# First half's layer norm by token, its swishes in other buffers, one projection and the bias rows moved

## The chip, the cores and the metric

The kernel runs on one core of a Trainium2 chip. The metric is the device time of one execution in microseconds (us): of the kernel before, three runs took 2139.2 (median), 2138.27 and 2141.2. The core has a matrix engine (TensorE, PE in the profile, with PEld for its weight loads), VectorE (DVE), ScalarE (ACT), GpSimd (POOL), and SyncE (SP), whose queue issues the transfers between the core and the chip's memory. Each engine works through its own list of instructions in order and waits at an instruction until what it needs is there; an instruction that waits holds up all behind it on that engine.

## The reference, cut to what matters

The model has two layers over 1024 tokens of 1024 features. Layer 0 is a convolution module and a gated feed-forward net, layer 1 dilated attention and the same kind of net. The change is in the convolution module and in the preparation of a bias table for the attention:

```
def layernorm(x, g, b):
    x32 = x.astype(jnp.float32)
    mu = jnp.mean(x32, axis=-1, keepdims=True)
    xc = x32 - mu
    var = jnp.mean(xc * xc, axis=-1, keepdims=True)
    y = xc * lax.rsqrt(var + EPS) * g.astype(jnp.float32) + b.astype(jnp.float32)
    return y.astype(x.dtype)

def conformer_conv(h, w_pw1, b_pw1, w_dw, b_dw, ln_g, ln_b, w_pw2, b_pw2):
    u = h @ w_pw1 + b_pw1
    a, gate = jnp.split(u, 2, axis=-1)
    u = a * jax.nn.sigmoid(gate)
    u = lax.conv_general_dilated(
        u, w_dw[:, None, :], window_strides=(1,), padding=[(CONV_WIDTH - 1, 0)],
        dimension_numbers=("NWC", "WIO", "NWC"), feature_group_count=CONV_CHANNELS) + b_dw
    u = jax.nn.silu(layernorm(u, ln_g, ln_b))
    return u @ w_pw2 + b_pw2
...
    bias = jnp.transpose(bias_table[t5_bucket(dist * dilation)], (2, 0, 1)).astype(jnp.float32)
...
    for i in range(DEPTH):
        h = rmsnorm(x, norm_mix[i])
        ...
        h = rmsnorm(x, norm_ffn[i])
        x = x + swiglu(h, ffn_w_gate[i], ffn_w_up[i], ffn_w_down[i])
```

## The kernel before, in words

All activations stand with features on the 128 partitions and tokens along the free axis, so a sum over features is a sum over partitions and over eight tiles. The 1024 tokens are worked in two halves of 512 (h = 0 and 1). Each projection is a `gemm`: weights and inputs are each split into a high and a low part, and three matmuls (lines 158, 159, 160) are issued for each of the eight blocks of 128 features, so one output tile takes 24 matmuls of 512 columns. Weights come through the SP queue (line 140), ACT casts the high part (line 127) and DVE or POOL subtract the low one (line 128).

The part that matters runs in this order in the code. `glu(1, c)` is the first projection with its gate for block c of the second half: two output tiles, 48 matmuls, then a sigmoid on ACT (line 382) and a product on DVE (line 389). `conv(0)` filters the first half: 31 taps, most on DVE (line 427), some on ACT and POOL (lines 418, 419), its sums in buffers called `ap` (four of them). `layernorm(0)` norms over the eight tiles `u` of the first half. `glu(1, 4)` is the last of those projections. `bias_rows` makes the rows of the attention's bias for three head groups. `pw2(0)` is the second projection of the first half, eight output tiles, 192 matmuls, added into x at line 504. Then comes the norm before the feed-forward net (`rstd`, lines 189 to 211, and `normed`, line 214) and the net itself, whose matmuls on the first half run beside `conv(1)`, the filter of the second half.

In `layernorm(0)` PE sums the eight tiles with a matrix of ones, which leaves each token's mean on all partitions (line 449, fp32, two passes each); DVE takes it off (line 451); ACT squares (line 472) into two buffers `ctmp` that take turns; PE sums the squares in the same way (line 473); ACT takes the root of a full tile (line 475) and DVE its reciprocal (line 479); DVE multiplies (line 483), ACT makes the swish into the two `ctmp` buffers (line 485), and DVE and POOL split it into high and low (lines 493, 495). `rstd` does it by token: DVE adds the squares (line 203), PE sums them into one column per 128 tokens (line 181, `colsum`), ACT and DVE work on 128x4 numbers (lines 208, 210), and PE spreads the four columns out again with an identity matrix (line 189, `rows`).

`bias_rows` does three times: load a one-hot table into a buffer `tmp` (SP, line 627), copy the heads' values beside it (DVE, line 630), one matmul (PE, line 632), negate the result into a second `tmp` (DVE, line 634), and write it out in 16 small transfers (SP, line 638), from which the attention reads its table later, from 1084.9 us on. There are four buffers `tmp`, handed out in the order of the code; the squares and the normed tiles of the feed-forward net's norm use the same four.

A scheduler orders the instructions of each engine by a model of their times, within the dependencies; `tc.issue_after(i)` puts the instructions of its block that run on the engine of i behind i on that engine. Before, `bias_rows` has its matmuls behind the last matmul of `glu(1, 4)`.

Of the kernel before, what the change touches and what calls it, by code (L numbers as in the profile page):

```python
# [12 lines left out]
F32 = mybir.dt.float32  # L13
F32R = mybir.dt.float32r
AF = mybir.ActivationFunctionType
ALU = mybir.AluOpType

P = 128
T = 1024
TH = 512  # L20
D = 1024
DC = D // P
# [64 lines left out]
def trunk(ctx, tc, xT, vecs, wdw, w1, w2, wqkv, wo, wg, wu, wd, rel, onehot, sel, outT, scratch, kept1):  # L87
    nc = tc.nc
# [7 lines left out]
    spool = ctx.enter_context(tc.tile_pool(name="spool", bufs=2))  # L96
# [6 lines left out]
    ones = const.tile([P, P], F32, name="ones")  # L103
    nc.vector.memset(ones, 1.0)
    epst = vec[:, NV : NV + 1]
# [44 lines left out]
    marks = {}  # L150
# [42 lines left out]
    def rstd(get, n, sc, pool=()):  # L193

        acc = sc.acc()[:, :n]
        for c in range(DC):
            sq = acc if c == 0 else sc.tmp()[:, :n]
            if c in pool:
                nc.gpsimd.tensor_tensor(out=sq, in0=get(c), in1=get(c), op=ALU.mult)
            else:  # L200
                nc.scalar.activation(sq, get(c), AF.Square)
            if c:
                nc.vector.tensor_tensor(out=acc, in0=acc, in1=sq, op=ALU.add)
        st = sc.st()
        colsum(st, acc, n)
        nj = n // P
        sd = spool.tile([P, 4], F32, name="sd")
        nc.scalar.activation(sd[:, :nj], st[:, 0:nj], AF.Sqrt, bias=epst, scale=1.0 / D)
        rs = spool.tile([P, 4], F32, name="rs")
        nc.vector.reciprocal(rs[:, :nj], sd[:, :nj])  # L210
        return rows(rs[:, :nj], n, sc)
# [108 lines left out]
    def conv_and_half_ffn():  # L320

        with ExitStack() as cs:
            cpool = cs.enter_context(tc.tile_pool(name="cpool", bufs=2))
# [45 lines left out]
            def glu(h, c, hl, bc=None, w=None):  # L369

                wb, wa = w or pw1_weights(c, True)
                pb = mm_ps()
                gemm(pb, wb, pairs(hl))
                pa = mm_ps()
                gemm(pa, wa, pairs(hl))
                if bc is not None:
                    tb, ta = tmp(), tmp()
                    nc.vector.tensor_tensor(out=tb, in0=pb, in1=bc, op=ALU.mult)
                    nc.vector.tensor_tensor(out=ta, in0=pa, in1=bc, op=ALU.mult)
                    pb, pa = tb, ta  # L380
                sg = tmp()
                nc.scalar.activation(sg, pb, AF.Sigmoid, bias=vec[:, V_B1 + DC + c : V_B1 + DC + c + 1])
                t = cpool.tile([P, KW - 1 + TH], F32, name="u", bufs=14)
                u[h, c] = t
                if h == 0:
                    nc.gpsimd.memset(t[:, : KW - 1], 0.0)
                else:
                    nc.scalar.copy(t[:, : KW - 1], u[0, c][:, TH:])
                nc.vector.scalar_tensor_tensor(
                    out=t[:, KW - 1 :],  # L390
                    in0=pa,
                    scalar=vec[:, V_B1 + c : V_B1 + c + 1],
                    in1=sg,
                    op0=ALU.add,
                    op1=ALU.mult,
                )
# [42 lines left out]
            def layernorm(h, sl, y):  # L439

                n = sl.stop - sl.start
                sc = csc[h]
                yh, yl = y
                vs = [u[h, c][:, sl] for c in range(DC)]
                if h == 0:

                    bc = sc.ps()[:, :n]
                    for c in range(DC):
                        nc.tensor.matmul(bc, ones, vs[c], start=(c == 0), stop=(c == DC - 1))
                    for c in range(DC):  # L450
                        nc.vector.scalar_tensor_tensor(
                            out=vs[c], in0=bc, scalar=-1.0 / D, in1=vs[c], op0=ALU.mult, op1=ALU.add
                        )
                else:
                    sv = sc.acc()[:, :n]
                    nc.vector.tensor_tensor(out=sv, in0=vs[0], in1=vs[1], op=ALU.add)
                    for c in range(2, DC):
                        nc.vector.tensor_tensor(out=sv, in0=sv, in1=vs[c], op=ALU.add)
                    st = sc.ps()
                    colsum(st, sv, n)  # L460
                    mu = spool.tile([P, 4], F32, name="mu")[:, : n // P]
                    nc.vector.tensor_scalar(
                        out=mu, in0=st[:, : n // P], scalar1=1.0 / D, scalar2=None, op0=ALU.mult
                    )
                    bc = rows(mu, n, sc)
                    for c in range(DC):
                        nc.vector.tensor_tensor(out=vs[c], in0=vs[c], in1=bc, op=ALU.subtract)
                if h == 0:
                    ps = sc.ps()[:, :n]
                    for c in range(DC):  # L470
                        sq = sc.tmp()[:, :n]
                        nc.scalar.activation(sq, vs[c], AF.Square)
                        nc.tensor.matmul(ps, ones, sq, start=(c == 0), stop=(c == DC - 1))
                    br = sc.acc()[:, :n]
                    root = nc.scalar.activation(br, ps, AF.Sqrt, bias=epst, scale=1.0 / D)
                    with tc.issue_after(root.ins):

                        nc.scalar.activation(spool.tile([P, 4], F32, name="sd")[:, 0:1], epst, AF.Silu)
                    nc.vector.reciprocal(br, br)
                else:  # L480
                    br = rstd(lambda c: vs[c], n, sc)
                for c in range(DC):
                    nc.vector.tensor_tensor(out=vs[c], in0=vs[c], in1=br, op=ALU.mult)
                    t = sc.tmp()[:, :n]
                    nc.scalar.activation(
                        t,
                        vs[c],
                        AF.Silu,
                        bias=vec[:, V_LNB + c : V_LNB + c + 1],
                        scale=vec[:, V_LNG + c : V_LNG + c + 1],  # L490
                    )
                    if h == 0:
                        nc.vector.tensor_copy(yh[:, c, sl], t)  # L493
                        eng = nc.vector if c % 2 else nc.gpsimd
                        eng.tensor_tensor(out=yl[:, c, sl], in0=t, in1=yh[:, c, sl].bitcast(F32), op=ALU.subtract)
                    else:
                        split(t, yh[:, c, sl], yl[:, c, sl], nc.vector if c % 2 else nc.gpsimd)
# [61 lines left out]
            conv(0, range(4))  # L559
            layernorm(0, whole, y)  # L560
            for c in range(LATE[0], LATE[1]):
                glu(1, c, hb)
            with tc.issue_after(marks["gemm"]):
                bias_rows()
            pw2(0, whole, y)
            for c in range(LATE[1], JOINT):
                glu(1, c, hb)
            ha = pair_slots()
# [783 lines left out]
```

## Time and profile before

| What | Value |
|---|---|
| Runs: median (lowest, highest) | 2139.2 us (2138.27, 2141.2) |
| Profiled execution: its time | 2142.52 us |
| Profiled execution: span of the instructions | 2140.7 us |
| Mean granted clock of TensorE | 0.988 of full speed |
| Busy share of PE, DVE, ACT, POOL | 97%, 63%, 39%, 25% |
| Chain that ended last, share by engine | PE 79%, DVE 9%, POOL 7% |

The profiled execution took 1.82 us more than its span and 3.32 us more than the median of the runs shown. The busy shares are averages; PE is busy nearly all the time, so what matters is where it isn't, and where it runs at the lower of its two clocks.

### The profile page before, as it was taken

What the parts mean: (1) busy time and instruction counts of PE and PEld (TensorE: products, weight loads), DVE (VectorE), ACT (ScalarE), POOL (GpSimd) and SP (SyncE); (2) the same over time, 40 slices, a digit from 0 to 9 for tenths busy, and PEclk for the clock granted to TensorE, in tenths of its full rate; (3) what the DMA queues carried; (4) which work ended last, traced back from release to release, by engine and by line L of the source; (5) the groups of instructions that cost most, each with busy time, mean ns of one, the idle gap of its engine ahead of it and who ended that gap; (6) DMA issues with size and microseconds to landing.
All of it is one profiled execution on the core that took longest, in us unless ns stands there. A gap on an engine that the chain in (4) does not pass through costs nothing.

```text
span 2140.7 us, 24625 instructions
## 1 busy us (share of the span) xinstructions
PE 2079.0 (97%) x9550; PEld 1681.0 (79%) x9550; DVE 1358.1 (63%) x1997; ACT 831.7 (39%) x1336; POOL 526.9 (25%) x322
## 2 busy tenths in 40 slices
PE   8999889999999999999999999999999999999997
PEld 6786677778887888888887777877888888888887
DVE  8997687997455433332663337489766666666665
ACT  6675366524323222211443434455322232222234
POOL 3984169921323222211230112130000000000003
PEclk9999899999999999999999999999999999999999
DMA  8232222222222223321231211122111111111112
GB/s 323 74 110 93 86 68 86 89 91 96 99 98 84 95 98 99 98 79 50 79 109 60 70 60 62 45 74 77 59 60 59 50 50 60 50 49 42 58 59 79
DMA packets 54778, 172.62 MB, mean 81 GB/s; under 512 B 6782, under 2 KB 12165, under 8 KB 54661
## 3 DMA queue, kind: packets, MB, share of 16 engines
q1 hardware_dynamic: 54084, 170.52, 24.0%
q8 instruction: 75, 1.23, 0.2%
q10 hardware_dynamic: 576, 0.52, 0.1%
q14 instruction: 43, 0.34, 0.1%
HBM read 159.22 MB, written 11.80 MB: 80 GB/s over the span
## 4 chain that ended last, share of the span: by engine, by line
PE 79%; DVE 9%; POOL 7%; issue 3%; ACT 2%; DMA 1%; SPq 0%; DVEq 0%; POOLq 0%; ACTq 0%
PE mm L158 12%; PE mm L160 12%; PE mm L159 12%; PE aux L158 6%; PE aux L160 6%; PE aux L159 6%; POOL ap L419 5%; PE mm L1031 4%; PE mm L1029 4%; PE mm L1030 4%; DVE cacc L427 2%; PE nps L1029 2%; PE nps L1030 2%; PE nps L1031 2%; PE att L768 1%
## 5 line engine op out<-in xcount | busy, mean ns | idle before, releaser
L158 PE MATMUL mm<-slot,wh 128*128 128x512 f32 x1184 | 467.5, 395 | 11.8 <-DVE slot L493 10.2
L159 PE MATMUL mm<-slot,wl 128*128 128x512 f32 x1184 | 465.9, 394 | 3.7 <-DVE wl L128 3.7
L160 PE MATMUL mm<-slot,wh 128*128 128x512 f32 x1184 | 462.4, 392 | 1.3 <-DVE slot L128 1.2
L128 POOL TENSOR_TENSOR wl<-ws,wh 128x1024 fp32r<-128x1024 f32 (+1 forms) x91 | 215.5, 2368 | 799.0 <-ACT wh L127 767.6
L127 ACT CAST wh<-ws 128x1024 fp32r<-128x1024 f32 (+1 forms) x190 | 195.6, 1030 | 346.2 <-PE mm L160 159.4
L158 PEld LDWEIGHTS mm<-slot,wh 128*128 128x128 f32 x1184 | 224.1, 189 | 64.7 <-DVE slot L493 12.1
L159 PEld LDWEIGHTS mm<-slot,wl 128*128 128x128 f32 x1184 | 224.1, 189 | 52.3 <-DVE wl L128 4.5
L160 PEld LDWEIGHTS mm<-slot,wh 128*128 128x128 f32 x1184 | 223.6, 189 | 49.5 <-DVE slot L128 2.1
L419 POOL TENSOR_TENSOR ap<-ap,m 128x512 f32<-128x512 f32 x156 | 224.7, 1474 | 55.2 <-ACT m L418 55.1
L128 DVE TENSOR_TENSOR wl<-ws,wh 128x1024 fp32r<-128x1024 f32 (+1 forms) x99 | 130.6, 1319 | 153.6 <-ACT wh L127 153.3
L427 DVE SCALAR_TENSOR_TENSOR cacc<-u,wd_sb,cacc 128x512 f32<-128x512 f32 x302 | 207.8, 743 | 0.1
L128 POOL TENSOR_TENSOR slot<-ws,slot 128x1024 fp32r<-128x1024 f32 x2 | 4.8, 2414 | 639.2 <-ACT slot L127 639.2
L158 PE MATMUL aux<-slot,wh 128*128 128x512 f32 x352 | 139.7, 397 | 7.7 <-DVE x L317 7.7
L418 ACT ACTIVATE m<-u,wd_sb 128x512 f32<-128x512 f32 x156 | 111.0, 722 | 77.4 <-POOL ap L419 77.2
L1029 PE MATMUL mm<-slot,wp 128*128 128x512 f32 x352 | 137.9, 392 | 2.8 <-DVE tmp L1095 2.3
L159 PE MATMUL aux<-slot,wl 128*128 128x512 f32 x352 | 138.7, 394 | 0.8 <-DVE wl L128 0.5
L160 PE MATMUL aux<-slot,wh 128*128 128x512 f32 x352 | 138.8, 394 | 0.0
L1030 PE MATMUL mm<-slot,wp 128*128 128x512 f32 x352 | 138.0, 392 | 0.2 <-DVE wp L128 0.2
L1031 PE MATMUL mm<-slot,wp 128*128 128x512 f32 x352 | 137.4, 392 | 0.0
L127 ACT CAST wp<-ws 128x512 fp32r<-128x512 f32 x110 | 67.8, 621 | 147.8 <-PE mm L1031 55.2
L946 DVE TENSOR_TENSOR x<-aux,x 128x512 f32<-128x512 f32 x144 | 98.3, 687 | 38.2 <-PE aux L160 37.0
L128 DVE TENSOR_TENSOR slot<-tmp,slot 128x512 fp32r<-128x512 f32 x58 | 95.6, 1651 | 29.9 <-ACT slot L127 29.7
(275 smaller groups left out, 3789.8 us busy)
## 6 DMA issues: line engine op xcount, KB each, us to landing
ws<-wd SPq DMA_DIRECT2D x66, 512.0 KB, 3.5
ws<-wu SPq DMA_DIRECT2D x64, 512.0 KB, 3.5
ws<-wg SPq DMA_DIRECT2D x62, 512.0 KB, 3.5
ws<-w SPq DMA_DIRECT2D x40, 512.0 KB, 4.8
ws<-wqkv SPq DMA_DIRECT2D x34, 512.0 KB, 3.5
ws<-wo SPq DMA_DIRECT2D x16, 384.0 KB, 3.0
kept<-slot SPq DMA_DIRECT2D x10, 512.0 KB, 6.0
ws<-kept SPq DMA_DIRECT2D x10, 512.0 KB, 5.1
```

Of the source, the lines that this page charges most:

```text
L127: a = nc.scalar.copy(hi, src)
L128: b = eng.tensor_tensor(out=lo, in0=src, in1=hi.bitcast(F32), op=ALU.subtract)
L158: nc.tensor.matmul(ps, wh[:, sl], xh, start=(k == 0), stop=False)
L159: nc.tensor.matmul(ps, wl[:, sl], xh, start=False, stop=False)
L160: mm = nc.tensor.matmul(ps, wh[:, sl], xl, start=False, stop=(k == kt - 1))
L418: nc.scalar.activation(m, src(c, k), AF.Copy, scale=wk)
L419: nc.gpsimd.tensor_tensor(out=a, in0=a, in1=m, op=ALU.add)
L427: nc.vector.scalar_tensor_tensor(out=a if k or late else u[h, c][:, :TH], in0=src(c, k), scalar=wk, in1=b if k == nv - 1 else a, op0=ALU.mult,
L946: eng.tensor_tensor(out=out, in0=a, in1=b, op=op)
L1029: nc.tensor.matmul(ps, wh, xh, start=start and k == 0, stop=False, skip_group_check=not start)
L1030: nc.tensor.matmul(ps, wl, xh, start=False, stop=False, skip_group_check=not start)
L1031: nc.tensor.matmul(ps, wh, xl, start=False, stop=k == 3, skip_group_check=not start)
```

## The change

There are four parts. In `layernorm(0)` the deviation is taken through `rstd`, by token, as the second half has it; the eight squaring matmuls, the root and reciprocal of a full tile go. The swishes of the first half go into the four `ap` buffers that the filter has done with. The matmuls of `glu(1, 4)` are queued on PE behind the last matmul of the mean (`marks["mean"]`). `bias_rows` stands behind `pw2(0)` in the code, and its matmuls are queued behind the last matmul of `pw2(0)`.

```diff
@@ layernorm
                     bc = sc.ps()[:, :n]
                     for c in range(DC):
-                        nc.tensor.matmul(bc, ones, vs[c], start=(c == 0), stop=(c == DC - 1))
+                        mm = nc.tensor.matmul(bc, ones, vs[c], start=(c == 0), stop=(c == DC - 1))
+                    marks["mean"] = mm.ins
...
-                if h == 0:
-                    ps = sc.ps()[:, :n]
-                    for c in range(DC):
-                        sq = sc.tmp()[:, :n]
-                        nc.scalar.activation(sq, vs[c], AF.Square)
-                        nc.tensor.matmul(ps, ones, sq, start=(c == 0), stop=(c == DC - 1))
-                    br = sc.acc()[:, :n]
-                    root = nc.scalar.activation(br, ps, AF.Sqrt, bias=epst, scale=1.0 / D)
-                    with tc.issue_after(root.ins):
-
-                        nc.scalar.activation(spool.tile([P, 4], F32, name="sd")[:, 0:1], epst, AF.Silu)
-                    nc.vector.reciprocal(br, br)
-                else:
-                    br = rstd(lambda c: vs[c], n, sc)
+                br = rstd(lambda c: vs[c], n, sc)
                 for c in range(DC):
                     nc.vector.tensor_tensor(out=vs[c], in0=vs[c], in1=br, op=ALU.mult)
-                    t = sc.tmp()[:, :n]
+                    t = cpool.tile([P, TH], F32, name="ap", bufs=4)[:, :n] if h == 0 else sc.tmp()[:, :n]
@@ conv_and_half_ffn
             layernorm(0, whole, y)
             for c in range(LATE[0], LATE[1]):
-                glu(1, c, hb)
+                with tc.issue_after(marks["mean"]):
+                    glu(1, c, hb)
+            pw2(0, whole, y)
             with tc.issue_after(marks["gemm"]):
                 bias_rows()
-            pw2(0, whole, y)
```

In the changed file the lines behind stand 1 to 12 lower: the multiplication is line 471, the swish 473, the split 481 and 483, the addition into x 492, and the bias rows' load, copy, matmul, negation and writes are lines 616, 619, 621, 623 and 627.

On SP the list changes between the weights of `pw2(0)` (`ws<-w`) and those of the net (`wg`, `wu`); `tmp<-onehot` is the load of a bias table, `scratch<-tmp` the writes of its rows:

```order
 L140 DMA ws<-w 128x1024 x5
-L627 DMA tmp<-onehot 33x384 x2
-L638 DMA scratch<-tmp 32x384 x32
-L627 DMA tmp<-onehot 33x384
-L638 DMA scratch<-tmp 32x384 x16
+L616 DMA tmp<-onehot 33x384
 L140 DMA ws<-w 128x1024 x3
```

The 48 writes and two of the loads went from ahead of the last weights of `pw2(0)` to behind the net's first four weights, where the list now has:

```order
+L616 DMA tmp<-onehot 33x384
+L627 DMA scratch<-tmp 32x384 x32
+L616 DMA tmp<-onehot 33x384
+L140 DMA ws<-wg 128x1024
+L627 DMA scratch<-tmp 32x384 x16
 L140 DMA ws<-wu 128x1024
```

The third table's load stands behind 32 writes. On DVE, at the end of `pw2(0)`, the kernel before has the last additions into x and the sum of squares `ssq` of the net's norm in turns:

```order
192 L504 SCALAR_TENSOR_TENSOR x_0_96<-mm,vec,x_0_96 128x512
193 L203 TENSOR_TENSOR ssq<-ssq,tmp 128x512
194 L504 SCALAR_TENSOR_TENSOR x_0_98<-mm,vec,x_0_98 128x512
195 L128 TENSOR_TENSOR wl<-ws,wh 128x1024
196 L203 TENSOR_TENSOR ssq<-ssq,tmp 128x512
197 L504 SCALAR_TENSOR_TENSOR x_0_100<-mm,vec,x_0_100 128x512
198 L203 TENSOR_TENSOR ssq<-ssq,tmp 128x512
199 L210 RECIPROCAL rs<-sd 128x4
```

The changed kernel has at the same place, from the last two additions into x on (`tmp<-aux` is the negation of a bias row, `tmp<-vec` the copy of the heads):

```order
185 L492 SCALAR_TENSOR_TENSOR x_0_98<-mm,vec,x_0_98 128x512
186 L128 TENSOR_TENSOR wl<-ws,wh 128x1024
187 L492 SCALAR_TENSOR_TENSOR x_0_100<-mm,vec,x_0_100 128x512
188 L623 TENSOR_SCALAR tmp<-aux 128x384
189 L619 COPY tmp<-vec 33x128
190 L623 TENSOR_SCALAR tmp<-aux 128x384
191 L619 COPY tmp<-vec 33x128
192 L623 TENSOR_SCALAR tmp<-aux 128x384
193 L203 TENSOR_TENSOR ssq<-ssq,tmp 128x512 x7
```

All seven additions of the squares went behind the three negations. On PE the three bias matmuls went from among the squares' matmuls (two of them) and the first matmuls of `pw2(0)` (one) to the place between the last matmul of `pw2(0)` and the `colsum` of the net's norm:

```order
954 L160 MATMUL mm<-slot,wh 128x512
955 L621 MATMUL aux<-tmp 128x384 x3
956 L181 MATMUL aux<-ones,ssq 128x1 x4
957 L189 MATMUL aux<-ident,rs 128x128 x4
958 L158 MATMUL mm<-slot,wh 128x512
```

## Rows read from the trace of the kernel before

**Rows 1.** Timeline of PE: start, length, instruction, [idle before, what ended it].

```profile
196.41 1.02 PE L449 MATMUL aux<-u,ones 128*128 128x512 f32 x2
200.04 1.02 PE L449 MATMUL aux<-u,ones 128*128 128x512 f32 x2
209.11 4.81 PE L473 MATMUL aux<-ctmp,ones 128*128 128x512 f32 x10
224.12 0.79 PE L158 MATMUL mm<-slot,wh 128*128 128x512 f32 x1 [10.20 <-DVE slot L493]
226.12 1.65 PE L632 MATMUL aux<-tmp 33*128 33x384 f32 x2
```

**Rows 2.** The same, from the end of `pw2(0)` to the net's first matmul.

```profile
272.50 0.39 PE L160 MATMUL mm<-slot,wh 128*128 128x512 f32 x1
277.04 1.87 PE L181 MATMUL aux<-ones,ssq 128*128 128x1 f32 x8 [4.15 <-DVE ssq L203]
279.47 2.08 PE L189 MATMUL aux<-ident,rs 128*128 128x128 f32 x8 [0.57 <-DVE rs L210]
283.04 0.80 PE L158 MATMUL mm<-slot,wh 128*128 128x512 f32 x1 [1.49 <-ACT slot L127]
```

**Rows 3.** Windows: length, busy of PE, PEld, DVE, ACT, POOL; PE's granted clock; DMA.

```profile
224.00:233.00 9.00, 8.88 (x19) 5.85 (x20) 7.34 (x12) 4.61 (x6) 4.18 (x4) 0.52 0.16 40
233.00:273.00 40.00, 39.89 (x176) 32.67 (x175) 19.89 (x22) 11.28 (x16) 3.36 (x2) 1.00 0.32 103
283.00:287.30 4.30, 4.26 (x10) 3.40 (x11) 4.30 (x7) 3.09 (x5) 3.98 (x3) 0.51 0.00 0
360.00:470.00 110.00, 99.70 (x416) 80.20 (x415) 110.00 (x140) 46.48 (x63) 71.53 (x42) 0.95 0.27 88
```

**Rows 4.** Timeline of DVE in `layernorm(0)` and in the bias rows.

```profile
195.41 0.69 DVE L437 TENSOR_TENSOR u<-cacc,ap 128x512 f32<-128x512 f32 x1
201.09 4.87 DVE L451 SCALAR_TENSOR_TENSOR u<-aux,u 128x512 f32<-128x512 f32 x8 [4.87 <-PE aux L449]
218.17 4.90 DVE L483 TENSOR_TENSOR u<-u,csv 128x512 f32<-128x512 f32 x8
228.40 0.55 DVE L634 TENSOR_SCALAR tmp<-aux 128x384 f32<-128x384 f32 x1
```

**Rows 5.** Timeline of DVE: additions of squares in a row, and the end of `pw2(0)`.

```profile
19.55 1.41 DVE L203 TENSOR_TENSOR ssq<-ssq,tmp 128x512 f32<-128x512 f32 x2
272.93 0.75 DVE L504 SCALAR_TENSOR_TENSOR x<-mm,vec,x 128x512 f32<-128x512 f32 x1 [2.48 <-PE mm L160]
281.58 2.72 DVE L214 SCALAR_TENSOR_TENSOR tmp<-x,vec,aux 128x512 f32<-128x512 f32 x4 [2.17 <-PE aux L189]
```

**Rows 6.** Timeline of PE early in the kernel, `colsum` and `rows` at the full clock.

```profile
25.27 0.95 PE L181 MATMUL aux<-ones,ssq 128*128 128x1 f32 x8
28.49 1.05 PE L189 MATMUL aux<-ident,rs 128*128 128x128 f32 x8
```

**Rows 7.** PE by lines from 224.3 to 272.7: count, busy us, mean ns.

```profile
L158 PE MATMUL mm<-slot,wh 128*128 128x512 f32 x64 | 26.7, 417 | 10.2 <-DVE slot L493 10.2
```

**Rows 8.** Timeline of SP's queue: start, length, transfers issued.

```profile
207.05 14.69 SPq L638 DMA_DIRECT2D scratch<-tmp  x32
221.83 0.32 SPq L627 DMA_DIRECT2D tmp<-onehot  x1
```

**Rows 9.** Transfers by line: count, KB each, median us from issue to landing.

```profile
scratch<-tmp SPq DMA_DIRECT2D x48, 48.0 KB, 1.6
```

**Rows 10.** Timeline of ACT between the squares and the root.

```profile
212.76 1.28 ACT L475 ACT_TABLE_LOAD   x1
214.06 0.69 ACT L475 ACTIVATE csv<-aux,vec 128x512 f32<-128x512 f32 x1
```

**Rows 11.** PE's waits: us in total, times, the longest.

```profile
PE aux L158 <- DVE x L317: 7.7, 2, 4.1
```

**Rows 12.** Timeline of DVE: three filter taps of `conv(1)` in a row.

```profile
383.48 2.06 DVE L427 SCALAR_TENSOR_TENSOR cacc<-u,wd_sb,cacc 128x512 f32<-128x512 f32 x3
```

## The prediction

> **What bounds the kernel now.** I read the timeline of PE first, since PE is busy nearly all the time and everything it doesn't do is seen as a gap there. Around the change it has two. At 224.12 the first matmul of `pw2(0)` waited 10.20 us for the cast of the first swish [rows 1]; the norm's chain through ACT and DVE stands in that gap. At 277.04 the `colsum` of the net's norm waited 4.15 us for DVE's last addition, and the net's first matmul came only at 283.04, though PE's last work had ended at 272.50 + 0.39 = 272.89 [rows 2]. The windows come second: after each gap PE runs at the lower clock (0.52 of full in the 9 us from 224, 0.51 in the 4.3 us from 283), and between them at full clock, with 176 matmuls in 39.89 us, 0.227 us each [rows 3]. So this stretch is bound by PE's work plus two chains that it waits for, and the change alters both chains. The third view is SP's queue: 32 writes of the bias rows took it 14.69 us, 0.46 us each, though one lands 1.6 us after its issue [rows 8, 9]. In the kernel before nobody waits for them.
>
> **The mean and the last first projection.** The last filter sum is done at 195.41 + 0.69 = 196.10 [rows 4]. Before, the two passes of the mean's last matmul began only at 200.04, behind matmuls of `glu(1, 4)`, and ended at 201.06 [rows 1]. Now nothing of `glu(1, 4)` is ahead of them: about 196.16 + 1.02 = 197.2, 3.9 us earlier. It isn't free: the matmuls that ran in between come afterwards, and PE idles for about 3 us in two pieces while it waits for the last two sums. All 48 of `glu(1, 4)` then run from 197.2 to 197.2 + 48 x 0.227 = 208.1, beside the norm, so PE's work is only moved. If the two pieces bring the lower clock, the 4.3 us at half speed from 283 say what that costs, about 2.1 us [rows 3]; the pieces are shorter than the 4.15 us that came before those, so I take nothing and keep 2.1 as the upper end.
>
> **The deviation by token.** DVE's eight subtractions take 4.87 us [rows 4], to 202.1. Seven additions follow at 0.72 (two took 1.41 with 0.69 for the second [rows 5]): 5.0 us, to 207.1, with ACT's squares in their shadow. That is before PE is free at 208.1, so `colsum` starts at 208.1. From `colsum` to the first use of the broadcast it was 281.58 - 277.04 = 4.54 us in the net's norm [rows 2, 5], at the lower clock; at the full one its two matmul groups take 0.95 and 1.05 instead of 1.87 and 2.08 [rows 2, 6], which leaves 2.6. PE comes here from unbroken work, so I take 2.9: the multiplications start at 211.0 (bounds 210.7 and 212.6), where they started at 218.17 [rows 4]. From there to PE's first matmul it was 224.12 - 218.17 = 5.95; DVE's list between is the same (eight multiplications, one product, a cast), so PE restarts at 217.0, 7.1 us earlier. The four buffers for the swishes bring the later tiles sooner, but PE was already busy for 8.88 of the 9 us after its restart [rows 3], so they are worth nothing beyond that; with two of them the cover would be the same slow clock.
>
> On the root there is a page to weigh. The row shows 1.28 us for the load of a table and the root 0.02 us behind it [rows 10]. The Trainium skill (ScalarE: Activation LUTs, What ACT_TABLE_LOAD costs) puts a drain of about 1.38 us on top of the load at every switch. By that the root would be some 0.5 us later and the whole 0.5 us longer; the row shows no such drain, and the sum goes by the row.
>
> **The second projection.** It is 3 x 64 = 192 matmuls (one of the three equal lines is shown [rows 7]), 192 x 0.227 = 43.6 us. Before, it lasted from 224.12 to 272.89 = 48.8, of which 1.65 was a bias matmul [rows 1]; so 3.6 us went to the lower clock. The bias matmul goes; I keep the 3.6, since a gap of similar length precedes (bounds 2.1, as after 283, and 4.3). `pw2(0)` then ends at E = 217.0 + 43.6 + 3.6 = 264.2, 8.7 us earlier.
>
> **The bias rows behind it.** Here a wait is added, and it is the largest term. From E: DVE's last addition into x takes 0.04 + 0.75 [rows 5], the first negation 0.55 [rows 4], so the first write is issued at E + 1.4. The second table was loaded ahead and its negation comes before SP needs it. 32 writes take SP 14.69 us [rows 8], to E + 16.1; only then does SP issue the third table's load. With the writes' 1.6 us to landing [rows 9] as the nearest row it is there at E + 17.8. PE stands at the third bias matmul, in front of its own `colsum`; that matmul takes 1.65 at the lower clock [rows 1], to E + 19.4, and the negation 0.55, to E + 20.0. Behind it on DVE stand all seven additions of the squares, 5.0 us: `colsum` at E + 25.1. (On ACT the squares wait too: the first two `tmp` they take are those whose writes must land, the second's at about E + 17.3, the third the one that the third bias matmul reads. So even without DVE's order the norm would start no earlier than that.) Before, it was E + 4.15 [rows 2]. From `colsum` to the net's first matmul I keep 283.04 - 277.04 = 6.0: the third group's 16 writes land by about E + 29, before the normed tile that takes their buffer. So the net starts at E + 31.1 = 295.3, where it started at 283.04: 12.3 us later. The cover of the bias rows before was 40 us of `pw2(0)`; it is gone.
>
> The Trainium skill (DMA: Bandwidth & Descriptors, Issuing engines are not separate DMA queues) says that what the sequencer spends on starting a DMA is usually small beside the DMA itself. Here one start is 0.46 and one landing 1.6 us, but 32 starts in a row are 14.69 and hide the landings, so rows and page differ in what counts. By the page the time would come out as the first rival.
>
> **Behind it.** `conv(1)`, its taps and the net move together, since both start from this norm. In the new order of DVE most of the net's instructions stand two taps earlier against `conv(1)`, 2 x 0.69 = 1.4 us [rows 12]. DVE is full from 360 to 470 and PE waits for it there (7.7 us for additions into x alone [rows 11]; 10.3 us idle in all [rows 3]), so PE may get back 0 to 4.5; I take 1. Nothing else in the rest moves but names of buffers and a few matmuls where PE had no gap.
>
> **The sum.** -8.7 to the end of `pw2(0)`, then 31.1 to the net's start instead of 10.15 (+21.0), -1.0: +11.3. The profiled execution took 2142.52, so 2153.8 by its own time; it is 3.32 above the median of the runs shown (2139.2), so I say 2150.5.
>
> **Rivals.** First: starting a write costs next to nothing when the queue has nothing else, and only landings count. Then the first negation is at E + 1.4, the second at 3.1, its writes land at 4.7 with the third table; matmul 0.9, negation 0.55, additions 5.0, `colsum` at E + 11.2 and the net at E + 17.2 = 281.4. That is -1.6 and -1.0 behind it: 2136.6, no change. For it: a write's data is only 48 KB. Against it: 0.46 us held through 32 writes in a row. 5%.
>
> Second, on the faster side: the bias rows hide here too, as their 48 writes did before, and the net's norm starts 10.15 us after E as it did. Then only the gain of the layer norm stands: -8.7 - 1.0, which gives 2129.5. It needs the third negation to be done before the additions are due, that is SP's 32 writes out by E; they can't begin before the first bias matmul, which stands behind the last of `pw2(0)`. From 11.3 us less of stall on, the change would be a gain. 7%.
>
> Third: the layer norm gives nothing back. The idle pieces at the mean drop the clock, `glu(1, 4)` and the chain run slow, and PE restarts about 224 as before; the stall of 21.0 then stands alone, with 1.0 back: 2159. For it: the clock fell after both gaps of rows 1 and 2. Against it: DVE's and ACT's chain is shorter whatever the clock. 6%.
>
> **How the numbers follow.** The forecast has 82%. Its own range: 2150.5 less 1.5 (shorter time at the lower clock), 3.5 (more given back behind) and 1 (landings), and plus 1.6 and 2.1 (slow clock in the chain and at the mean), 0.7 and 2 (longer slow stretches): not all at once, so 2144 to 2157. That leaves out the three rivals and the ends, 2 in 10. A measurement of this kernel tells 0.2%, about 4.3 us, from no change: faster than 2134.9 is the second rival, 7%; within is the first and the lowest end of the forecast, 6%; slower 87%.
>
> **What would show it.** PE: the mean's last matmul ends near 197, `pw2(0)` starts near 217 and ends near 264; a gap of about 16 us before the third bias matmul and one before `colsum`, and the net's first matmul near 295. SP: 32 writes of 0.46 us begin 1.4 us after `pw2(0)` and the third load stands behind them. DVE: seven additions behind the third negation. It is wrong if the third load lands before E + 10, if `colsum` comes under 15 us after `pw2(0)`, or if PE restarts after 221.

## The result and the profile after

The changed kernel took 2154.06 us (median of four runs, 2153.13 to 2154.93), the kernel before beside it 2140.2 (2138.27 to 2142.54): a ratio of 1.0062, 95% interval 1.0049 to 1.0075. It is slower by 13.9 us. The forecast was 2150.5, with 2144 to 2157 as its range. The profiled execution of the changed kernel took 2153.13 us, span 2151.3, mean granted clock 0.983; by profiled executions it is +10.6 over 2142.52, where the prediction had +11.3 and 2153.8. Of the two profiled executions the one before was the slowest of its four and the one after the fastest of its four, so the medians lie further apart than these two do.

First PE's timeline (start, length, instruction, [idle before, what ended it]), to be read beside [rows 1, 2]:

```profile
191.76 1.12 PE L449 MATMUL aux<-u,ones 128*128 128x512 f32 x2 [1.56 <-DVE u L437]
194.80 1.31 PE L449 MATMUL aux<-u,ones 128*128 128x512 f32 x2 [1.92 <-DVE u L437]
...
196.33 0.63 PE L159 MATMUL mm<-slot 128*128 128x512 f32 x1
...
208.30 0.95 PE L181 MATMUL aux<-ones,csv 128*128 128x1 f32 x8
209.91 1.13 PE L189 MATMUL aux<-ident,rs 128*128 128x128 f32 x8 [0.66 <-DVE rs L210]
217.08 0.76 PE L158 MATMUL mm<-slot,wh 128*128 128x512 f32 x1 [6.05 <-DVE slot L481]
...
263.21 0.39 PE L160 MATMUL mm<-slot,wh 128*128 128x512 f32 x1
263.53 0.91 PE L621 MATMUL aux<-tmp 33*128 33x384 f32 x2
267.28 1.60 PE L621 MATMUL aux<-tmp 33*128 33x384 f32 x2 [2.84 <-DVE tmp L619]
281.65 1.62 PE L621 MATMUL aux<-tmp 33*128 33x384 f32 x2 [12.78 <-DMA tmp<-onehot]
289.29 1.87 PE L181 MATMUL aux<-ones,ssq 128*128 128x1 f32 x8 [6.02 <-DVE ssq L203]
...
295.29 0.80 PE L158 MATMUL mm<-slot,wh 128*128 128x512 f32 x1 [1.49 <-ACT slot L127]
```

Down to 263.21 everything is earlier than before: the gap of 10.20 us at 224.12 is one of 6.05 at 217.08, and `pw2(0)` ends at E = 263.21 + 0.39 = 263.60 instead of 272.89. Then come gaps of 2.84, 12.78 and 6.02 us, where there was one of 4.15 [rows 2], and the net starts at 295.29 instead of 283.04: 12.25 us later.

What stands behind the two longest of them shows on SP's queue, on ACT and on DVE, each a timeline of the same stretch. SP:

```profile
265.06 14.70 SPq L627 DMA_DIRECT2D scratch<-tmp  x32
279.86 0.32 SPq L616 DMA_DIRECT2D tmp<-onehot  x1
```

ACT, the first three squares that the net's norm adds up:

```profile
273.63 0.63 ACT L201 ACTIVATE tmp<-x 128x512 f32<-128x512 f32 x1 [8.96 <-DMA scratch<-tmp]
281.05 0.63 ACT L201 ACTIVATE tmp<-x 128x512 f32<-128x512 f32 x1 [6.79 <-DMA scratch<-tmp]
283.31 0.63 ACT L201 ACTIVATE tmp<-x 128x512 f32<-128x512 f32 x1 [1.62 <-PE aux L621]
```

DVE, the filter's last sum, then the norm's subtractions, additions and multiplications, then the end of the projection:

```profile
194.06 0.69 DVE L437 TENSOR_TENSOR u<-cacc,ap 128x512 f32<-128x512 f32 x1
196.15 4.87 DVE L452 SCALAR_TENSOR_TENSOR u<-aux,u 128x512 f32<-128x512 f32 x8 [1.40 <-PE aux L449]
...
211.07 4.87 DVE L471 TENSOR_TENSOR u<-u,aux 128x512 f32<-128x512 f32 x8 [1.31 <-PE aux L189]
...
264.95 2.23 DVE L619 COPY tmp<-vec 33x128 f32<-33x128 f32 x1
268.92 0.56 DVE L623 TENSOR_SCALAR tmp<-aux 128x384 f32<-128x384 f32 x1 [1.74 <-PE aux L621]
269.39 0.21 DVE L619 COPY tmp<-vec 33x128 f32<-33x128 f32 x1
283.31 0.56 DVE L623 TENSOR_SCALAR tmp<-aux 128x384 f32<-128x384 f32 x1 [13.71 <-PE aux L621]
283.78 5.46 DVE L203 TENSOR_TENSOR ssq<-ssq,tmp 128x512 f32<-128x512 f32 x7
```

The 32 writes keep SP for 14.70 us, as they did before [rows 8], and the third load stands behind them; PE's wait of 12.78 ends with it. The seven additions stand in one row behind the third negation. In the kernel before, six of them were done one by one inside the projection, and only the seventh behind it; that is the one for which PE waited 4.15 us [rows 2].

Last the windows (length, then busy us of PE, PEld, DVE, ACT and POOL with counts, the granted clock, DMA):

```profile
195.60:199.00 3.40, 3.40 (x9) 2.44 (x8) 2.85 (x5) 1.83 (x3) 0.00 (x0) 0.50 0.00 0
217.00:226.00 9.00, 8.92 (x27) 7.16 (x28) 8.93 (x12) 3.04 (x4) 5.54 (x4) 0.67 0.01 2
264.00:295.00 31.00, 7.60 (x22) 4.55 (x20) 10.41 (x16) 7.01 (x11) 2.34 (x1) 0.55 0.34 95
372.00:482.00 110.00, 102.03 (x427) 82.72 (x426) 109.89 (x144) 48.02 (x64) 71.48 (x43) 0.95 0.27 91
```

The first begins in the mean's last matmul and goes on into `glu(1, 4)`, at half the clock. In 31 us after the projection PE is busy for 7.60. In the filter's stretch, 12 us later than in [rows 3], PE does 102.03 us of work in 110 where it did 99.70. From the net's first matmul to the end of the span it is 1856.0 instead of 1857.7: 1.65 us of the 12.25 come back. How far this is the change's doing is taken up below.

### The profile page after: what moved, and what is told of

Its sections match the earlier page's. It is cut to its first block, busy times and chain, and to the rows that moved or that the text cites. A ratio compares the mean times of both kernels' runs of the same rounds, so it can differ in the third digit from the quotient of the medians.

```text
span 2151.3 us, 24634 instructions
## 1 busy us (share of the span) xinstructions
PE 2074.5 (96%) x9550; PEld 1681.2 (78%) x9550; DVE 1355.4 (63%) x2004; ACT 831.2 (39%) x1335; POOL 526.1 (24%) x322
## 4 chain that ended last, share of the span: by engine, by line
PE 75%; DVE 15%; POOL 4%; issue 3%; DMA 2%; SPq 1%; ACT 1%; DVEq 0%; POOLq 0%; ACTq 0%
PE mm L158 11%; PE mm L160 10%; PE mm L159 10%; DVE cacc L427 7%; PE aux L158 6%; PE aux L159 6%; PE aux L160 6%; PE mm L1018 4%; PE mm L1020 4%; PE mm L1019 4%; POOL ap L419 2%; DVE slot L128 2%; PE nps L1019 2%; PE nps L1018 2%; PE nps L1020 2%
## 5 line engine op out<-in xcount | busy, mean ns | idle before, releaser
L159 PEld LDWEIGHTS mm<-slot,wl 128*128 128x128 f32 x1184 | 224.3, 189 | 50.5 <-DVE wl L128 2.8
```

Source lines behind the costliest of these rows:

```text
L159: nc.tensor.matmul(ps, wl[:, sl], xh, start=False, stop=False)
```

## The experiments

The theory on test has two halves. The layer norm's part of the change gains about 8 us. The bias rows behind the projection lose some 20, because the net's norm waits for them in two ways: PE stands at a third bias matmul whose table comes late, and the squares get no buffer until the rows have theirs. In the text below E is always the end of `pw2(0)`'s last matmul in the kernel spoken of. The stall from E to the net's first matmul was 10.15 us before [rows 2] and is 31.7 after.

**e1, the bias rows ahead of the projection again, all else changed**

```
             for c in range(LATE[0], LATE[1]):
                 with tc.issue_after(marks["mean"]):
                     glu(1, c, hb)
-            pw2(0, whole, y)
             with tc.issue_after(marks["gemm"]):
                 bias_rows()
+            pw2(0, whole, y)
```

> The changed kernel with the bias rows put back ahead of the second projection, where the kernel before has them; the other three parts of the change stay. Theory A (the loss is the stall between the second projection and the net's norm, the layer norm's parts are a gain of about 9 us): the second projection ends near 265, colsum follows about 4 us later as before, the net's first matmul near 275.5 instead of 295.3; 2134.3 us, 6 us under the kernel before (2140.2). Rival B (the loss lies in the layer norm's parts, such as the idle time at the mean, and the bias rows only show it): no gain from the move, about 2154.

Measured: 2135.59, ratio to before 0.9976 (0.9966 to 0.9985). The rest of the change is a gain; its place is the layer norm. In its trace the net starts 80.2 us after the filter's last sum (278.00 - 197.82), in the kernel before 86.9 (283.04 - 196.10): 6.7 us less. The 8 us of the theory hold 1.65 that are not the norm's, the bias matmul that left the projection [rows 1]; here it is back ahead of it.

**e2, the kernel before with the bias rows moved behind the projection and nothing else**

```
             layernorm(0, whole, y)
             for c in range(LATE[0], LATE[1]):
                 glu(1, c, hb)
+            pw2(0, whole, y)
             with tc.issue_after(marks["gemm"]):
                 bias_rows()
-            pw2(0, whole, y)
```

> The kernel before with only the bias rows moved behind the second projection. Theory A: the second projection ends 2 us earlier (no bias matmul in it), then the stall of about 21.5 us comes in; the net starts near 302.5 instead of 283.0; 2158.7 us. Rival B: the move costs nothing by itself, about 2140.

Measured: 2159.03, ratio 1.0087 (1.0073 to 1.0101). The stall from E to the net is 31.7 us here as well (268.51 to 300.20), with the same gaps in front of the second and third bias matmul and `colsum` (2.79, 12.78 and 6.03), so it has nothing to do with the other parts. With e1 the two halves add up: -5.2 and +18.3 make +13.1, and the whole change measured +13.9.

**e3, the changed kernel with four wide writes in place of each sixteen**

```
-                for i in range(HPG):
-                    n = P // HPG
-                    nc.sync.dma_start(scratch[g, h, i * n : (i + 1) * n], br[h * n : (h + 1) * n])
+                n = P // HPG
+                nc.sync.dma_start(
+                    scratch[g, h].rearrange("(i r) c -> r i c", i=HPG),
+                    br[h * n : (h + 1) * n].unsqueeze(1).broadcast_to([n, HPG, 3 * P]),
+                )
```

> The changed kernel with each group's 16 writes of 48 KB made 4 writes of 192 KB, the same bytes in a quarter of the issues. Theory A (SP's issues of 0.46 us each are the stall): 8 instead of 32 issues ahead of the third table's load; the second negation, at 5.9 us behind the second projection, then counts; third load lands at about 9.7, colsum about 17.4 us behind the second projection instead of 25.7: 8.3 us less, 2145.8 us. Rival C (bytes or landings count, not issues): no change, 2154.

Measured: 2150.48 (2142.06 to 2152.05), ratio 1.004 (1.0028 to 1.0051); the profiled execution took 2148.05. That is between the two expectations. SP's queue shows that it was held by the number of starts and not by the bytes:

```profile
266.42 2.27 SPq L626 DMA_DIRECT2D scratch<-tmp  x4
268.73 0.85 SPq L616 DMA_DIRECT2D tmp<-onehot  x1
270.82 2.23 SPq L626 DMA_DIRECT2D scratch<-tmp  x4
```

Four starts of 192 KB take 2.27 us, 0.57 each where one of 48 KB took 0.46, and the third load goes out at 268.73 instead of 279.86. PE in the same stretch:

```profile
264.56 0.39 PE L160 MATMUL mm<-slot,wh 128*128 128x512 f32 x1
...
271.72 1.61 PE L621 MATMUL aux<-tmp 33*128 33x384 f32 x2 [1.53 <-DMA tmp<-onehot]
280.55 1.87 PE L181 MATMUL aux<-ones,ssq 128*128 128x1 f32 x8 [7.21 <-DVE ssq L203]
...
286.55 0.80 PE L158 MATMUL mm<-slot,wh 128*128 128x512 f32 x1 [1.49 <-ACT slot L127]
```

The wait for the load falls from 12.78 to 1.53, that for the additions rises from 6.02 to 7.21: the squares wait for the writes to land, and a wide write lands 3.7 us after its issue (median), a small one 1.6. The net starts at E + 21.6, so 10.1 us of the stall are gone, more than theory A's 8.3. The time moved by 3.6 (medians) to 5.1 (profiled executions) only. In the profiled one 1.3 us had been lost before the filter's last sum (196.05 against 194.75), and the rest from the net to the end took 1859.8 instead of 1856.0. A window there:

```profile
363.00:473.00 110.00, 99.41 (x412) 79.86 (x412) 110.00 (x143) 47.38 (x64) 71.10 (x42) 0.95 0.26 86
```

In the filter's stretch, where DVE is full, PE did 2.6 us less work than in the changed kernel. DVE's list is not the same there: at 295.19 it has eleven filter taps in a row ahead of the net's next weights, where the changed kernel, at 303.93, has nine. No run shows whether that is the reason, and why it fell out so stays open. What the run does settle is that starts, not bytes, held the load back.

**e4, the bias rows where the change put them, tables and rows in buffers of their own**

```
+            free = [csc[0].tmp, csc[0].tmp, csc[0].acc]
             with tc.issue_after(marks["gemm"]):
-                bias_rows()
+                bias_rows(lambda: cpool.tile([P, TH], F32, name="ap", bufs=4), lambda: free.pop(0)())
...
-    def bias_rows():
+    def bias_rows(table=tmp, row=tmp):
...
+        tables = [table()[: NBK + 1] for _ in range(NG)]
+        for g in range(NG):
+            nc.sync.dma_start(tables[g][:, : 3 * P], onehot[g])
         for g in range(NG):
-            both = tmp()[: NBK + 1]
+            both = tables[g]
...
-            nc.sync.dma_start(oh, onehot[g])
...
-            br = tmp()[:, : 3 * P]
+            br = row()[:, : 3 * P]
```

> The changed kernel; the bias rows stay behind the second projection, but all three tables are loaded ahead into three of the four ap buffers, and the negated rows go into the two ctmp buffers and csv, so that the squares of the net's norm find their tmp buffers free. Theory A: the three bias matmuls lie in the 4 us that PE waits for the last sum of squares, DVE's additions run beside the second projection again; the net starts about 10 us behind the second projection, near 273.6: 2132.4 us, 7.8 under the kernel before. Theory A without the buffers' part (only the third load's place counts): the same. Rival D (the 48 writes themselves disturb what runs beside them, the weights' loads behind them on SP above all): the net's matmuls wait for weights some 25 to 35 us behind the second projection, 2138 or more.

Measured: 2133.96, ratio 0.9968 (0.9957 to 0.998), faster than both kernels. PE:

```profile
266.36 0.39 PE L160 MATMUL mm<-slot,wh 128*128 128x512 f32 x1
266.68 2.20 PE L624 MATMUL aux<-ap 33*128 33x384 f32 x6
270.91 1.87 PE L181 MATMUL aux<-ones,ssq 128*128 128x1 f32 x8 [2.03 <-DVE ssq L203]
...
276.91 0.80 PE L158 MATMUL mm<-slot,wh 128*128 128x512 f32 x1 [1.49 <-ACT slot L127]
```

All three bias matmuls run in a row inside the wait for the last addition, and the net starts at E + 10.2, as in the kernel before. So the place behind the projection isn't what costs; the waits that it brought are. The 48 writes themselves, still behind the projection, cost little: in the 63 us from the net's start PE waits once, 1.4 us, for a weight's low part, where e1 has no such wait; rival D wanted several times that. The next two runs take them apart.

**e5, only the tables ahead, the rows still in `tmp`**

```
             with tc.issue_after(marks["gemm"]):
-                bias_rows()
+                bias_rows(lambda: cpool.tile([P, TH], F32, name="ap", bufs=4))
...
-    def bias_rows():
+    def bias_rows(table=tmp):
...
+        tables = [table()[: NBK + 1] for _ in range(NG)]
+        for g in range(NG):
+            nc.sync.dma_start(tables[g][:, : 3 * P], onehot[g])
         for g in range(NG):
-            both = tmp()[: NBK + 1]
+            both = tables[g]
...
             br = tmp()[:, : 3 * P]
```

> The changed kernel with one difference: all three bias tables are loaded ahead, into three of the filters' buffers; the negated rows stay in the tmp buffers. This takes away the late third load and keeps the squares of the net's norm queued behind the rows. E is the end of the second projection; in the changed kernel the net starts at E + 31.7. Theory A (two waits, one inside the other: the squares get their tmp buffers only after the rows, so all seven stand behind the second projection; and the third load stands behind 32 writes): the squares go one by one through the one tmp buffer that is left, 0.63 for the square and 0.70 for the addition with two hand-overs of 0.04, 1.4 each, from about E + 2.8; colsum at E + 12.5, net at E + 18.5, 13.2 earlier than in the changed kernel: 2141. Theory B (only the third load costs, the squares would be done in time): net at E + 8.5 as in e4, 2134. Theory C (the writes hold the buffers and the squares wait for their landings): as slow as the changed kernel, 2154 or more.

Measured: 2141.08, ratio 1.0 (0.999 to 1.001). Theory A, within a microsecond. ACT after the projection:

```profile
265.04 0.63 ACT L201 ACTIVATE tmp<-x 128x512 f32<-128x512 f32 x1
268.13 0.63 ACT L201 ACTIVATE tmp<-x 128x512 f32<-128x512 f32 x1 [2.47 <-DVE ssq L203]
269.52 0.63 ACT L201 ACTIVATE tmp<-x 128x512 f32<-128x512 f32 x1 [0.76 <-DVE ssq L203]
```

One square every 1.39 us but for the last, each waiting for the addition in front of it and none for a landing: the rows hold three buffers, and the single one that is left goes round. `colsum` comes at 275.89 (E + 11.8) and the net at E + 17.8.

**e6, as e4, with the third load alone put back behind the 32 writes**

```
-        for g in range(NG):
+        for g in range(2):
             nc.sync.dma_start(tables[g][:, : 3 * P], onehot[g])
...
+            if g == 2:
+                with tc.issue_after(w.ins):
+                    nc.sync.dma_start(oh, onehot[g])
...
-                    nc.sync.dma_start(scratch[g, h, i * n : (i + 1) * n], br[h * n : (h + 1) * n])
+                    w = nc.sync.dma_start(scratch[g, h, i * n : (i + 1) * n], br[h * n : (h + 1) * n])
```

> The other half of the pair: as e4 (tables and rows in buffers of their own, so the squares are done within the second projection), but the third table's load is put back behind the 32 writes of the first two groups. Theory A (two waits): SP is at it at E + 16.1, it lands near E + 18, PE stands at the third bias matmul in front of colsum, which comes near E + 19.5 and the net near E + 25.5, 6.2 earlier than in the changed kernel (E + 31.7): 2148. Theory D (only the squares' place costs, the late load is hidden): 2134 as e4. Theory E (the late load is the whole of it): 2154.

Measured: 2148.5, ratio 1.0034 (1.0021 to 1.0048). PE:

```profile
263.75 0.39 PE L160 MATMUL mm<-slot,wh 128*128 128x512 f32 x1
264.06 1.55 PE L627 MATMUL aux<-ap 33*128 33x384 f32 x4
282.23 1.61 PE L627 MATMUL aux<-ap 33*128 33x384 f32 x2 [16.61 <-DMA ap<-onehot]
283.77 1.86 PE L181 MATMUL aux<-ones,ssq 128*128 128x1 f32 x8
...
289.77 0.80 PE L158 MATMUL mm<-slot,wh 128*128 128x512 f32 x1 [1.49 <-ACT slot L127]
```

Here the additions were done long before (the last ended at 268.23), and `colsum` follows the third bias matmul at once, at E + 19.6; the net starts at E + 25.6. The four stalls are 10.2 (neither wait, e4), 17.8 (the squares' alone), 25.6 (the load's alone) and 31.7 (both). The sum of the two extras is 7.6 + 15.4 = 23.0, both together make 21.5: they stand nearly end to end, since the additions are queued on DVE behind the negation that waits for the load. The times follow: 2133.96, 2141.08, 2148.5 and 2154.06.

**e9, only the rows in other buffers, the three tables left in `tmp`**

```
+            free = [csc[0].tmp, csc[0].tmp, csc[0].acc]
             with tc.issue_after(marks["gemm"]):
-                bias_rows()
+                bias_rows(lambda: free.pop(0)())
...
-    def bias_rows():
+    def bias_rows(row=tmp):
...
-            br = tmp()[:, : 3 * P]
+            br = row()[:, : 3 * P]
```

> The changed kernel with the negated rows alone in buffers of their own (two ctmp and the free csv); the three tables stay in the tmp buffers and nothing is put ahead by hand. E is the end of the second projection. Theory A (the third load was late because its tmp buffer was one that the rows had ahead of it): with no rows in tmp the third table gets a buffer during the first half's norm, its load goes out then, one tmp buffer is left for the squares within the projection, and both waits are gone: colsum near E + 4, net near E + 10, 2134 as e4. Rival (the load's place behind the writes on SP's queue follows from its place in the program, whatever the buffers): 2148 as with the late third load.

Measured: 2134.93, ratio 0.9972 (0.996 to 0.9984). SP's third load, then PE:

```profile
218.68 0.29 SPq L617 DMA_DIRECT2D tmp<-onehot  x1
...
264.93 0.39 PE L160 MATMUL mm<-slot,wh 128*128 128x512 f32 x1
...
275.42 0.80 PE L158 MATMUL mm<-slot,wh 128*128 128x512 f32 x1 [1.49 <-ACT slot L127]
```

Nothing was moved by hand, and yet the third load goes out at 218.68, during the layer norm, and the net starts at E + 10.1. Both waits thus came from one thing: the three rows stood in the four `tmp` buffers, which are handed out in the order of the code, and took the ones that the third table and the squares needed.

**e10, e7 and e8, the parts of the layer norm, each undone by itself on top of e1**

e10 has the swishes in `ctmp` again:

```
-                    t = cpool.tile([P, TH], F32, name="ap", bufs=4)[:, :n] if h == 0 else sc.tmp()[:, :n]
+                    t = sc.tmp()[:, :n]
```

> The bias rows ahead of the second projection (as e1, 2135.6), and the first half's swishes back in the two ctmp buffers: that part of the change undone by itself. Theory A (the second projection starts with the first tiles, and runs at the lower clock for its first microseconds, so that later tiles are in time with two buffers too): 2135 to 2137. Rival (with two buffers the third swish waits for the first tile's subtraction and the later tiles come late; each one pushes the projection back): 2139 or more.

Measured: 2135.29, ratio 0.9972 (0.9961 to 0.9983), as e1. The four buffers for the swishes are worth nothing.

e7 has `glu(1, 4)` in its old place:

```
             for c in range(LATE[0], LATE[1]):
-                with tc.issue_after(marks["mean"]):
-                    glu(1, c, hb)
+                glu(1, c, hb)
```

> The bias rows ahead of the second projection (as e1, 2135.6), and glu(1, 4) not queued behind the mean: that part of the change undone by itself. Theory A: TensorE has the same work between the last filter sum and colsum whichever way round it lies; in e1 colsum at 211.84 waits for the end of glu(1, 4) and not for the additions, which are done at 210.34; with the mean some 3 us later the additions end near 211.5 to 212.5 and colsum comes at the same time or up to 1 us later: 2135 to 2137. Rival: the 3 to 4 us by which the mean comes earlier are what the layer norm gains: 2139 or more.

Measured: 2136.93, ratio 0.9981 (0.9972 to 0.999): inside theory A by its time. Its trace doesn't go by my reason, though: PE waits 6.76 us for the additions in front of `colsum` and runs the chain at the lower clock (`colsum` 1.83 us, where it is 0.95 in e1), and the projection starts 27.4 us after the filter's last sum (222.86 - 195.49), in e1 23.9. The medians differ by 1.3 us and their intervals overlap; what the queueing behind the mean is worth lies between nothing and some 3 us, and stays open. This kernel is also the kernel before with the new deviation and the swishes' buffers alone, and those were worth nothing in e10: so the deviation, in the old order, takes some 4 us off by itself (2141.07 to 2136.93).

e8 has the old deviation:

```
-                br = rstd(lambda c: vs[c], n, sc)
+                if h == 0:
+                    ps = sc.ps()[:, :n]
+                    for c in range(DC):
+                        sq = sc.tmp()[:, :n]
+                        nc.scalar.activation(sq, vs[c], AF.Square)
+                        nc.tensor.matmul(ps, ones, sq, start=(c == 0), stop=(c == DC - 1))
...
+                    nc.vector.reciprocal(br, br)
+                else:
+                    br = rstd(lambda c: vs[c], n, sc)
```

> The bias rows ahead of the second projection (as e1, 2135.6), with the old deviation in the first half (eight full matmuls of squares, root and reciprocal over 128x512) and the rest of the change kept. Theory A: the deviation by token carries the gain, about 4 of e1's 5 us. The old chain's last square comes 17 us after the last filter sum as in the kernel before, where the first projection lay in front of the mean and lies between the squares now; from there to the multiplications 4.2 us: 2139 to 2141, no gain over the kernel before. Rival: the gain is that of the reordering, and this one stays at 2136.

Measured: 2147.95, ratio 1.0029 (1.0018 to 1.0041), 12 us slower than e1 and 7 slower than the kernel before. The reordering without the new deviation is no gain but a loss, so with e7 the gain is the deviation's; that without it one would be back at the kernel before, as theory A had it, does not hold. ACT shows why:

```profile
197.99 1.23 ACT L473 ACTIVATE ctmp<-u 128x512 f32<-128x512 f32 x2 [7.33 <-DVE u L452]
204.02 0.63 ACT L473 ACTIVATE ctmp<-u 128x512 f32<-128x512 f32 x1 [4.79 <-PE aux L474]
204.88 0.63 ACT L473 ACTIVATE ctmp<-u 128x512 f32<-128x512 f32 x1 [0.23 <-PE aux L474]
...
209.86 0.63 ACT L473 ACTIVATE ctmp<-u 128x512 f32<-128x512 f32 x1 [3.77 <-PE aux L474]
```

The old deviation needs PE after every second square, and `glu(1, 4)`, queued behind the mean, now lies between: after two squares ACT waits 4.79 us, then 3.77. The last squaring matmul ends 22.8 us after the filter's last sum (218.05 - 195.28), 17.8 in the kernel before (213.92 - 196.10 by [rows 1, 4]).

## Why the prediction was right

- The mean. It had 197.2, measured 194.80 + 1.31 = 196.1. The filter's last sum came 1.35 us earlier in this execution, ahead of anything that was changed. The lower clock, which was taken at nothing, did come: 0.50 from 195.6 to 199.0, where nine matmuls took 3.40 us, so about 1.7 us. The upper end had 2.1.
- The deviation by token. `colsum` 208.1, measured 208.30; multiplications 211.0, measured 211.07; restart of PE 217.0, measured 217.08. The mechanism held: PE's first projections, and not DVE's additions, came last in front of `colsum`. That the times agree to 0.2 us is partly luck: the early sum (1.35 us) and the lower clock that was not counted (about 1.7) nearly cancel. From the filter's last sum to `colsum` it is 13.55 us, forecast 12.0.
- The second projection. E = 264.2, measured 263.60: the slow clock cost 46.5 - 43.6 = 2.9 us where 3.6 was kept from before. Of the 9.3 us by which E came earlier than before, 7.9 lie behind the filter's last sum; the forecast had 8.7 there.
- The bias rows. First write E + 1.4, measured E + 1.46; third load after the 32 writes, E + 16.1 and E + 16.26; third matmul E + 17.8 and E + 18.05; end of its negation E + 20.0 and E + 20.3; `colsum` E + 25.1 and E + 25.7; net E + 31.1 and E + 31.7. The gap forecast as about 16 us came in two, 2.84 in front of the second bias matmul and 12.78 in front of the third, and ended at the same place. The seven additions took 5.46 us, 0.78 each, not 0.72, since most of the squares waited for the addition in front of them. The remark that ACT's squares wait for landings as well was right (8.96 and 6.79 us); e5 shows what the rows in `tmp` cost the squares where the load is not in the way, 7.6 us. What the text did not see is that the load's lateness comes from the same buffers (e9).
- The rule of the Trainium skill (DMA: Bandwidth & Descriptors, Issuing engines are not separate DMA queues), on which the first rival stood, does not decide here: one start of 0.46 us is small beside a landing of 1.6, but 32 starts in a row took 14.70 us, and e3 shows the load out as soon as there are fewer starts.
- Behind it. -1.0, measured -1.65. Its reason is not shown. From the net's first matmul to the end of the span the profiled executions of all twelve kernels took between 1855.7 and 1859.8 us; e1, without the longer stall, took 1855.8, and e2, with the stall alone, 1858.7. So what came back does not go with the stall, and the agreement of this term may be chance.
- The sum. +11.3, measured +10.6 by profiled executions: 2153.8 forecast by that clock, 2153.13 measured. The step to the median was wrong. The profiled execution of before was slower than the three runs shown, 3.32 above their median, and the text took that off; the profiled execution of the changed kernel was its fastest, 0.93 below its median. So the step was forecast as -3.3 and measured +0.9, 4.25 apart, and the 0.7 us by which the other terms were too high brings that to the 3.6 by which 2150.5 misses the median 2154.06. It is the mis-sized term. The medians alone say +13.9, and with the kernel before as it ran beside the experiments (medians 2140.76 to 2141.17) 12.9 to 13.3. Where the 2 to 3 us between these and the +10.6 of the two traces lie, two single traces can't show; that the terms agree so well owes something to the pair of executions that was profiled.

Of the rivals the first is shown false by SP's queue, the second (the rows hide) by the stall, though e9 shows how near it lay: with the rows in other buffers the net starts at E + 10.1, as it needed, and the change is a gain. The third (the layer norm gives nothing back) falls with e1.

## What to carry to other kernels

Before a step with its own buffers is moved, ask which pool it takes them from and who is next in line: a pool handed out in the order of the code makes a late user hold up work that doesn't depend on it, here a load and seven squares. Where a row of small transfers is issued by one queue, count the starts and not the bytes, and look what else stands in that queue. And take a forecast's base from a median or from the trace, but don't add the gap between the two to the result: it belongs to one execution.

## What the runs showed of the hardware

The copy of 33x128 on DVE takes 0.21 us at 269.39; at 264.95 it took 2.23, and POOL's timeline of the same stretch has a subtraction beside it that ends with it:

```profile
264.75 2.34 POOL L128 TENSOR_TENSOR wl<-ws,wh 128x1024 fp32r<-128x1024 f32 x1 [8.48 <-ACT wh L127]
```

In e4 the same subtraction falls on the last addition of two tiles, for which `colsum` waits there; it takes 2.10 us where one took 0.69 [rows 5]. In the kernel before it is so too: the addition that ends the wait of 4.15 us [rows 2] takes 2.40. DVE's timeline of e4:

```profile
268.75 2.10 DVE L203 TENSOR_TENSOR ssq<-ssq,tmp 128x512 f32<-128x512 f32 x1
```

That agrees with the Trainium skill (SBUF — State Buffer, Who interferes with whom), by which such a copy, and an instruction of VectorE with two inputs in SBUF, can be shut out for as long as one of GpSimd's runs. In the changed kernel it cost about 2.0 of the 2.84 us in front of the second bias matmul (2.23 less 0.21), and nothing in the end, since SP's writes lasted longer.
